# A recurrence stage without two-input work on GpSimd, and with its filler matmuls at fixed places

## The chip, the cores and the metric

The kernel runs on one core of a Trainium2 chip. The metric is the device time of one execution in microseconds (us); the median of three runs before the change is 2841.66 us (2840.65 to 2843.72). TensorE multiplies, VectorE, ScalarE and GpSimd work elementwise, and SyncE issues the DMAs. In rows of the profile they are PE (its weight loads PEld), DVE, ACT, POOL and SP.

## What is computed

One backbone layer over 1024 latent and 256 context tokens of width 1024: a half-step SwiGLU, two token mixers on one input projection, and a second half-step SwiGLU. The mixers are a softmax attention and a gated linear recurrence with 4 heads and two directions, over chunks of 64 tokens. The part that the change touches is the recurrence, cut here to what matters:

```python
def forget_gate(f_raw, lb):
    f = lb + (1.0 - lb) * sigmoid(f_raw)
    return 1.0 - f, log(f)                                  # k, g

b = cumsum(g, within each chunk)
ds = einsum('bnshk,bnshv->bnhkv', kc * exp(b_last - b), vc)  # per chunk
state = exp(b_last) * state + ds                             # from chunk to chunk
s = tril(einsum('bnchk,bnshk->bnhcs', qc * exp(b - b_mid), kc * exp(b_mid - b)))
o = einsum('bnhcs,bnshv->bnchv', s, vc) + einsum('bnchk,bnhkv->bnchv', qc * exp(b), s_prev)
o = rms_norm(o_forward + reversed(o_backward)) * silu(g_raw)
y = (sigmoid(p8) * (o_att @ w_att_out) + sigmoid(p9) * (o_hg @ w_hg_out)) @ w_o
```

## The kernel before

The layer runs as stages one behind another: first SwiGLU, input projections with attention, the recurrence stage, the merge of the two mixers, and second SwiGLU. Nearly all large products are done as three matmuls on a high and a low half of each operand (`term`, L98 to L102): a weight of 128x1024 is loaded by SyncE into one of three `st` buffers, `act.copy` makes the high half, and a subtraction makes the low half (`load_w`, L87 to L93). The engine of that subtraction (L92) is an argument.

The recurrence stage (L815 to L1040) takes each of 4 heads in 2 directions:

- `load_head` (L855 to L877) fetches a head's inputs and applies the sigmoids on ScalarE. GpSimd multiplies `g` by its sigmoid (L876).
- `prep` (L879 to L933) is the elementwise work of one direction: `fs` scaled on ScalarE (L880), `k` as one minus `fs` on GpSimd (L882), the logarithm on ScalarE, the scan on VectorE (L886 or L888), then exponentials on ScalarE and about fifteen products on VectorE, up to `b` (L930) and `qb` (L932).
- `mix` (L935 to L995) does the scores on TensorE (L941, L950), copies them under a mask into `ST` (L957), transposes (L968), forms chunk products (L977), and steps the state `Sp` on VectorE (L985), eight times one behind another.
- `head_out` (L997 to L1029) adds the two score tables on GpSimd (`both`, L1000), multiplies out the head's output on TensorE (L1008, L1010), normalises on VectorE, transposes (L1026), multiplies by `g` (L1028) and stores to `ohg_d`.

TensorE has little to do for a head itself. So the gate projections, which only the merge needs, are spread through the stage as fillers: 16 weight columns, each with two items of 24 matmuls of 128x512, 768 in all, written into `fb`, copied to `ft` on ScalarE and stored to `gate_d`. `Fillers.next` makes one item and asks for the weight of the next column; the pool of weight halves has 4 buffers, two columns. In the kernel before, `fill()` counts its calls and releases items in proportion (calls over 64); what is left is done by `fl.upto(1)` at the head of the merge stage. The tile framework orders the instructions of each engine from this program by priorities of its own; each engine then runs its own queue strictly in order.

The merge stage waits for both mixers: it reloads `oatt_d` and `ohg_d` through the same `st` buffers (L1060), splits them into halves (L1062, L1063), and multiplies with `w_mrg`.

Of the kernel before, what the change touches and what calls it, by code (L numbers as in the profile page):

```python
# [13 lines left out]
AF = mybir.ActivationFunctionType  # L14
ALU = mybir.AluOpType
# [37 lines left out]
def hybrid_block(ctx: ExitStack, tc: tile.TileContext, xT, cc, cols, w_mod, w_gate, w_up, w_down, w_tok, w_col,  # L53
# [765 lines left out]
    psF = out_ctx.enter_context(tc.tile_pool(name="ps3f", bufs=2, space=PSUM, reuse_waits="tile"))  # L819
    with tc.tile_pool(name="hg", bufs=1, reuse_waits="tile") as hp, \  # L820
            tc.tile_pool(name="psH", bufs=6, space=PSUM, reuse_waits="tile") as psH:
        fl = Fillers(wp, ep, psF, pool, False)
        for j in range(KT):
            fl.cols(B_GA, j, gate_d[0], (0, 1))
            fl.cols(B_GB, j, gate_d[1], (0, 1))
        calls = [0]

        def fill():
            calls[0] += 1
            fl.upto(calls[0] / 64)  # L830

        lower_bounds(hp.tile([P, 16], F32, name="lbr"))
        m01 = hp.tile([P, T + 1], BF16, name="m01")
# [21 lines left out]
        def load_head(h):  # L855
            rows = slice(h * P, (h + 1) * P)
            fs = []
            for d in range(2):
                t = hp.tile([P, T], F32, name="fs", bufs=3)
                sp.dma_start(out=t, in_=f_d[d][rows, :])  # L860
                fs.append(t)
            q = hp.tile([P, SEQ], F32, name="q", bufs=1)
            g = hp.tile([P, SEQ], F32, name="g", bufs=2)
            vt = hp.tile([P, NKT, P], F32, name="vt", bufs=2)
            sp.dma_start(out=q, in_=hq_d[rows, :])
            sp.dma_start(out=vt, in_=hv_d[:, rows].rearrange("(b p) d -> p b d", p=P))
            sp.dma_start(out=g, in_=hg_d[rows, :])
            table(fs[0], fs[0], AF.Sigmoid)
            sq = w4("sg", 1)
            table(sq, q, AF.Sigmoid)  # L870
            table(fs[1], fs[1], AF.Sigmoid)
            sg = w4("sg", 1)
            table(sg, g, AF.Sigmoid)
            tc.stamp_issue_order_token(act.preload_act_table_set("natural_log_exp_and_others").ins, "tables")
            dve.scalar_tensor_tensor(q, q, HG_SCALE, sq, op0=ALU.mult, op1=ALU.mult)
            pool.tensor_tensor(g, g, sg, op=ALU.mult)  # L876
            return fs, q, g, vt  # L877

        def prep(h, d, fs, q):  # L879
            act.activation(fs, fs, AF.Identity, scale=oml[:, d, h:h + 1], bias=lb[:, d, h:h + 1])  # L880
            k = hp.tile([P, T], F32, name="k", bufs=2)
            pool.tensor_scalar(k, fs, -1.0, 1.0, op0=ALU.mult, op1=ALU.add)  # L882
            table(fs, fs, AF.Ln)
            b = hp.tile([P, T], F32, name="b", bufs=2)
            if d == 0:
                dve.tensor_tensor_scan(b, m01[:, 0:T], fs, 0.0, op0=ALU.mult, op1=ALU.add)  # L886
            else:
                dve.tensor_tensor_scan(b[:, ::-1], m01[:, 1:T + 1][:, ::-1], fs[:, ::-1], 0.0,  # L888
                                       op0=ALU.mult, op1=ALU.add)
            mid, last = (31, 63) if d == 0 else (32, 0)  # L890
            b3 = b.rearrange("p (c t) -> p c t", t=CHUNK)
            x3 = b3[:, 0:16]
            fx = fs[:, 0:SEQ]
            dve.tensor_tensor(fx.rearrange("p (c t) -> p c t", t=CHUNK), x3,
                              x3[:, :, mid:mid + 1].broadcast_to([P, 16, CHUNK]), op=ALU.subtract)
            f, s_ = (0, 1) if d == 0 else (1, 0)

            dec = hp.tile([P, 52], F32, name="dec", bufs=2)
            em, el = dec[:, 20:36], dec[:, 36:52]
            dve.tensor_copy(dec[:, 0:20], b3[:, :, last])  # L900
            dve.tensor_copy(em, x3[:, :, mid])
            dve.tensor_tensor(el, dec[:, 0:16], em, op=ALU.subtract)
            bc = b3[:, 16:20]
            dve.tensor_tensor(bc, bc, dec[:, 16:20].unsqueeze(2).broadcast_to([P, 4, CHUNK]), op=ALU.subtract)
            act.activation(dec, dec, AF.Exp)
            qt = w4("qt")
            act.activation(qt, fx, AF.Exp)
            act.activation(fx, fx, AF.Exp, scale=-1.0)
            bx = b[:, SEQ:T]
            act.activation(bx, bx, AF.Exp, scale=-1.0)  # L910
            dec2 = hp.tile([P, 10], F32, name="dec2", bufs=2)
            dve.tensor_tensor(dec2, dec[:, 0:20:2], dec[:, 1:20:2], op=ALU.mult)
            dve.tensor_tensor(qt, qt, q, op=ALU.mult)
            dve.tensor_tensor(fx, fx, k[:, 0:SEQ], op=ALU.mult)
            dve.tensor_tensor(bx, bx, k[:, SEQ:T], op=ALU.mult)
            bf = bc[:, f::2]
            dve.tensor_tensor(bf, bf, dec[:, 16 + s_:20:2].unsqueeze(2).broadcast_to([P, 2, CHUNK]), op=ALU.mult)

            def wide(v, n):
                return v.unsqueeze(2).broadcast_to([P, n, CHUNK])  # L920

            k3, t3 = (t.rearrange("p (c t) -> p c t", t=CHUNK) for t in (fx, qt))
            q2 = hp.tile([P, 512], F32, name="q2", bufs=2)
            k1 = hp.tile([P, 512], F32, name="k1", bufs=2)
            dve.tensor_tensor(k1.rearrange("p (c t) -> p c t", t=CHUNK), k3[:, f::2], wide(el[:, f::2], 8), op=ALU.mult)
            dve.tensor_tensor(q2.rearrange("p (c t) -> p c t", t=CHUNK), t3[:, s_::2], wide(em[:, s_::2], 8),
                              op=ALU.mult)
            dve.tensor_tensor(el[:, f::2], el[:, f::2], dec[:, s_:16:2], op=ALU.mult)
            dve.tensor_tensor(em[:, s_::2], em[:, s_::2], dec[:, f:16:2], op=ALU.mult)
            dve.tensor_tensor(x3, k3, wide(el, 16), op=ALU.mult)  # L930
            qb = w4("qb", 3)
            dve.tensor_tensor(qb.rearrange("p (c t) -> p c t", t=CHUNK), t3, wide(em, 16), op=ALU.mult)  # L932
            return fx, qt, qb, b, q2, k1, dec2  # L933

        def mix(d, vt, fx, qt, qb, b, q2, k1, dec2):  # L935
            f, s_ = (0, 1) if d == 0 else (1, 0)
            ps = hbank()
            kr = slice(f * CHUNK, (f + 1) * CHUNK)
            for i in range(8):
# [46 lines left out]
                    state.append(nxt)  # L986

            kts = [to_tokens(groups[0])]
            fill()
            for j in range(3):  # L990
                if j < 2:
                    kts.append(to_tokens(groups[j + 1]))
                fill()
                update(groups[j], kts[j])
            return qb, Sp  # L995

        def head_out(h, vt, g, dirs):  # L997
            rows = slice(h * P, (h + 1) * P)
            both = hp.tile([P, 8, P], F32, name="both")
            pool.tensor_tensor(both, ST[0], ST[1], op=ALU.add)  # L1000
            ss = hp.tile([P, 8], F32, name="ss", bufs=2)
            pss = []
            for half in range(2):
                ps = hbank()
                for i in range(4):
                    bk = half * 4 + i
                    o = ps[:, i * P:(i + 1) * P]
                    pe.matmul(o, both[:, bk, :], vt[:, bk, :], start=True, stop=False)  # L1008
                    for d, (qb, Sp) in enumerate(dirs):
                        pe.matmul(o, qb[:, bk * P:(bk + 1) * P], Sp[:, bk, :], start=False, stop=(d == 1))  # L1010
                sq = hp.tile([P, 512], F32, name="sq", bufs=2)
                act.activation(sq, ps, AF.Square)
                dve.reduce_sum(ss[:, half * 4:half * 4 + 4], sq.rearrange("p (b e) -> p b e", e=P), axis=AX.X)
                pss.append((ps, sq))
            fill()
            r = hp.tile([P, 8], F32, name="rr", bufs=2)
            rsqrt(r, ss, P)
            for half, (ps, on) in enumerate(pss):
                dve.tensor_tensor(on.rearrange("p (b e) -> p b e", e=P), ps.rearrange("p (b e) -> p b e", e=P),
                                  r[:, half * 4:half * 4 + 4].unsqueeze(2).broadcast_to([P, 4, P]), op=ALU.mult)  # L1020
            fill()
            for half, (_, on) in enumerate(pss):
                cs_ = slice(half * 512, half * 512 + 512)
                ps = hbank()
                for i in range(4):
                    pe.transpose(ps[:, i * P:(i + 1) * P], on[:, i * P:(i + 1) * P], ident)  # L1026
                og = g[:, cs_]
                dve.scalar_tensor_tensor(og, ps, col[:, 120:121], og, op0=ALU.mult, op1=ALU.mult)  # L1028
                sp.dma_start(out=ohg_d[rows, cs_], in_=og)  # L1029

        for _ in range(4):
            fill()
        heads = [load_head(0)]
        ready = prep(0, 0, heads[0][0][0], heads[0][1])
        for h in range(HGH):
# [184 lines left out]
```

## Time and profile before

| | us |
|---|---|
| median of three runs | 2841.66 (2840.65 to 2843.72) |
| the profiled execution | 2842.11 |
| its span, first to last instruction | 2840.1 |
| PE busy | 2720.6 (96% of the span) |
| DVE busy | 1588.3 (56%) |
| ACT busy | 991.8 (35%) |
| POOL busy | 238.0 (8%) |

The mean granted TensorE clock is 0.985 of full speed. Busy shares are means over stages with different limits: the page's second part cuts the span into 40 slices of 71 us, and TensorE stands at nine tenths in most of them; in the three slices from about 1633 to 1846 us, inside the recurrence stage (about 1617 to 1902 us), it stands at eight, and VectorE at eight, eight and six. So the stage has to be read by itself.

### The profile page before, as it was taken

What the parts mean: (1) busy time and instruction counts of PE and PEld (TensorE: products, weight loads), DVE (VectorE), ACT (ScalarE), POOL (GpSimd) and SP (SyncE); (2) the same over time, 40 slices, a digit from 0 to 9 for tenths busy, and PEclk for the clock granted to TensorE, in tenths of its full rate; (3) what the DMA queues carried; (4) which work ended last, traced back from release to release, by engine and by line L of the source; (5) the groups of instructions that cost most, each with busy time, mean ns of one, the idle gap of its engine ahead of it and who ended that gap; (6) DMA issues with size and microseconds to landing.
All of it is one profiled execution on the core that took longest, in us unless ns stands there. A gap on an engine that the chain in (4) does not pass through costs nothing.

```text
span 2840.1 us, 37295 instructions
## 1 busy us (share of the span) xinstructions
PE 2720.6 (96%) x15032; PEld 2326.4 (82%) x15032; DVE 1588.3 (56%) x3053; ACT 991.8 (35%) x1463; POOL 238.0 (8%) x192
## 2 busy tenths in 40 slices
PE   4799999999999899999999988899999999999998
PEld 3588888888888798989988877788878888888887
DVE  7756544444434886566665488644495333333337
ACT  3521111111112443278776565344354211111122
POOL 4700000000000000200000132112000000000000
PEclk9899999999999999999999999999999999999999
DMA  6553223323211433311021333154353211111122
GB/s 230 178 160 90 76 73 89 97 76 96 62 43 56 145 116 112 99 45 36 29 66 34 93 131 127 65 192 138 115 175 115 70 45 45 45 52 52 45 79 92
DMA packets 115276, 261.56 MB, mean 92 GB/s; under 512 B 12320, under 2 KB 51872, under 8 KB 115104
## 3 DMA queue, kind: packets, MB, share of 16 engines
q1 hardware_dynamic: 115104, 259.18, 28.7%
q8 instruction: 118, 1.93, 0.3%
q14 instruction: 54, 0.44, 0.0%
HBM read 218.77 MB, written 40.37 MB: 91 GB/s over the span
## 4 chain that ended last, share of the span: by engine, by line
PE 82%; DVE 8%; issue 4%; ACT 3%; DMA 2%; POOL 1%; SPq 0%; DVEq 0%; ACTq 0%; POOLq 0%
PE bank L100 14%; PE bank L101 14%; PE bank L102 14%; PE y L100 6%; PE y L101 6%; PE y L102 6%; PE fb L102 3%; PE fb L101 3%; PE fb L100 3%; PE S L754 3%; PE bank L770 2%; PE po L783 1%; PE po L784 1%; PE qb L100 1%; PE qb L101 1%
## 5 line engine op out<-in xcount | busy, mean ns | idle before, releaser
L100 PE MATMUL bank<-uh,w 128*128 128x512 f32 (+1 forms) x1952 | 712.6, 366 | 19.9 <-ACT uh L457 15.0
L101 PE MATMUL bank<-ul,w 128*128 128x512 f32 (+1 forms) x1952 | 714.1, 366 | 6.8 <-POOL ul L458 6.8
L102 PE MATMUL bank<-uh,w 128*128 128x512 f32 (+1 forms) x1952 | 712.7, 365 | 0.3 <-DVE w L92 0.3
L91 ACT CAST w<-st 128x1024 fp32r<-128x1024 f32 x238 | 248.0, 1051 | 790.5 <-PE y L101 432.2
L100 PEld LDWEIGHTS bank<-uh,w 128*128 128x128 f32 x1952 | 369.1, 189 | 80.6 <-ACT uh L457 17.1
L101 PEld LDWEIGHTS bank<-ul,w 128*128 128x128 f32 x1952 | 369.6, 189 | 67.6 <-POOL ul L458 10.1
L102 PEld LDWEIGHTS bank<-uh,w 128*128 128x128 f32 x1952 | 370.2, 190 | 58.1 <-DVE w L92 0.8
L92 DVE TENSOR_TENSOR w<-st,w 128x1024 fp32r<-128x1024 f32 x216 | 263.8, 1230 | 239.7 <-ACT w L91 237.0
L352 DVE TENSOR_TENSOR y<-y,y 128x512 f32<-128x512 f32 (+1 forms) x416 | 254.8, 619 | 200.5 <-PE y L102 199.0
L100 PE MATMUL y<-h,w 128*128 128x512 f32 (+1 forms) x736 | 284.0, 388 | 10.8 <-DVE y L352 6.1
L101 PE MATMUL y<-h,w 128*128 128x512 f32 (+1 forms) x736 | 282.9, 385 | 0.0
L102 PE MATMUL y<-h,w 128*128 128x512 f32 (+1 forms) x736 | 281.5, 383 | 0.2
L337 DVE TENSOR_TENSOR sl<-bank,sl 128x512 f32<-128x512 f32 (+1 forms) x114 | 70.6, 620 | 369.8 <-PE bank L102 365.5
L100 PE MATMUL fb<-uh,w 128*128 128x512 f32 (+1 forms) x576 | 222.3, 386 | 0.3 <-ACT ft L112 0.3
L102 PE MATMUL fb<-uh,w 128*128 128x512 f32 (+1 forms) x576 | 219.6, 381 | 0.0
L101 PE MATMUL fb<-ul,w 128*128 128x512 f32 (+1 forms) x576 | 219.2, 380 | 0.0
L100 PEld LDWEIGHTS y<-h,w 128*128 128x128 f32 x736 | 139.1, 190 | 44.2 <-DVE y L352 10.0
L102 PEld LDWEIGHTS y<-h,w 128*128 128x128 f32 x736 | 139.5, 190 | 27.5 <-DVE w L92 1.0
L101 PEld LDWEIGHTS y<-h,w 128*128 128x128 f32 x736 | 139.8, 190 | 24.6 <-DVE h L339 0.2
L338 ACT CAST h<-sl 128x512 fp32r<-128x512 f32 (+1 forms) x92 | 55.3, 604 | 288.3 <-DVE sl L337 288.1
L336 ACT ACTIVATE sl<-bank 128x512 f32<-128x512 f32 (+1 forms) x114 | 61.2, 539 | 191.8 <-PE bank L102 191.3
L774 DVE TENSOR_TENSOR pl<-bank,ph 128x512 fp32r<-128x512 f32 x160 | 108.1, 684 | 29.4 <-ACT ph L773 29.4
(224 smaller groups left out, 4182.1 us busy)
## 6 DMA issues: line engine op xcount, KB each, us to landing
st<-in_w_mod SPq DMA_DIRECT2D x77, 512.0 KB, 3.7
st<-in_w_gate SPq DMA_DIRECT2D x56, 512.0 KB, 3.8
st<-in_w_up SPq DMA_DIRECT2D x56, 512.0 KB, 3.7
st<-in_w_down SPq DMA_DIRECT2D x56, 512.0 KB, 3.6
st<-in_w_col SPq DMA_DIRECT2D x36, 512.0 KB, 3.6
gate_d<-ft SPq DMA_DIRECT2D x32, 256.0 KB, 2.7
gt<-gate_d SPq DMA_DIRECT2D x32, 256.0 KB, 2.7
st<-in_w_o SPq DMA_DIRECT2D x16, 512.0 KB, 3.7
```

The costliest lines, as they stand in the source:

```text
L91: act.copy(hi, st)
L92: eng.tensor_tensor(lo, st, f32(hi), op=ALU.subtract)
L100: pe.matmul(ps, lh, rh, start=first, stop=False)
L101: pe.matmul(ps, lh, rl, start=False, stop=False)
L102: pe.matmul(ps, ll, rh, start=False, stop=last)
L336: act.activation(sl, pg, AF.Silu)
L337: dve.tensor_tensor(sl, pu, sl, op=ALU.mult)
L338: act.copy(hh, sl)
L352: dve.tensor_tensor(yd, py, yd, op=ALU.add)
L754: pe.matmul(S[:, cs_], qT[:, (s * 2 + t) * P:(s * 2 + t + 1) * P], kT[g][:, cs_], start=(s == 0), stop=(s == 1))
L770: pe.transpose(pt[:, (a * 2 + t) * P:(a * 2 + t + 1) * P], prob[t][:, kt * P:(kt + 1) * P], ident)
L774: dve.tensor_tensor(pl.rearrange("p a q -> p (a q)"), pt, f32(ph).rearrange("p a q -> p (a q)"), op=ALU.subtract)
```

## The change

Four operations of the recurrence stage leave GpSimd: the subtraction for filler weights (`Fillers` gets `dve`), the product `g`, and the sum `both` go to VectorE; `k` goes to ScalarE as an activation with scale -1 and bias 1. `fill` no longer counts; it makes one item, or as many as it is told. The calls stand at fixed places: four items ahead of the heads, one at the head of `mix`, one behind the masked copies, and two in `head_out` behind `both`. That is 4 + 16 + 8 = 28 items of 32; four remain for `fl.upto(1)`.

```diff
-        fl = Fillers(wp, ep, psF, pool, False)
+        fl = Fillers(wp, ep, psF, dve, False)
...
-        calls = [0]
-
-        def fill():
-            calls[0] += 1
-            fl.upto(calls[0] / 64)
+        def fill(n=1):
+            for _ in range(min(n, len(fl.todo))):
+                fl.next()
...
-            pool.tensor_tensor(g, g, sg, op=ALU.mult)
+            dve.tensor_tensor(g, g, sg, op=ALU.mult)
...
-            pool.tensor_scalar(k, fs, -1.0, 1.0, op0=ALU.mult, op1=ALU.add)
+            act.activation(k, fs, AF.Identity, scale=-1.0, bias=1.0)
...
         def mix(d, vt, fx, qt, qb, b, q2, k1, dec2):
             f, s_ = (0, 1) if d == 0 else (1, 0)
+            fill()
             ps = hbank()
...
             kts = [to_tokens(groups[0])]
-            fill()
             for j in range(3):
                 if j < 2:
                     kts.append(to_tokens(groups[j + 1]))
-                fill()
                 update(groups[j], kts[j])
...
-            pool.tensor_tensor(both, ST[0], ST[1], op=ALU.add)
+            dve.tensor_tensor(both, ST[0], ST[1], op=ALU.add)
+            fill(2)
...
-            fill()
             r = hp.tile([P, 8], F32, name="rr", bufs=2)
...
-            fill()
             for half, (_, on) in enumerate(pss):
...
-        for _ in range(4):
-            fill()
+        fill(4)
         heads = [load_head(0)]
```

How the queues change is shown at three places. On GpSimd, in the stage from the first head on, the kernel before has this (the first twelve rows of it; `w` is the low half of a filler weight):

```order
L876 TENSOR_TENSOR g<-g,sg 128x1024
L92 TENSOR_TENSOR w<-st,w 128x1024
L882 TENSOR_SCALAR k<-fs 128x1280
L92 TENSOR_TENSOR w<-st,w 128x1024
L876 TENSOR_TENSOR g<-g,sg 128x1024
L1000 TENSOR_TENSOR both<-ST_14480,ST_14481 128x1024
L882 TENSOR_SCALAR k<-fs 128x1280
L92 TENSOR_TENSOR w<-st,w 128x1024
L882 TENSOR_SCALAR k<-fs 128x1280
L92 TENSOR_TENSOR w<-st,w 128x1024
L876 TENSOR_TENSOR g<-g,sg 128x1024
L1000 TENSOR_TENSOR both<-ST_14480,ST_14481 128x1024
```

With the change, all that GpSimd has between the attention and the end of the merge is this:

```order
L832 MEMSET m_14470 128x1281
L842 MEMSET ST_14480 128x1024
L833 MEMSET m_14470 128x21
L842 MEMSET ST_14481 128x1024
L1077 TENSOR_TENSOR gt<-gt 128x512 x16
```

So GpSimd has no work at all beside the four heads. On VectorE, in the second head, behind the state of its first direction, the changed kernel has (`m` the chunk pattern of the scan, `s` and `Sp` the state, `dec` its decay):

```order
L874 TENSOR_TENSOR g<-g,sg 128x1024
L956 COPY_PREDICATED ST_14481<-mask_14474,hb 32x8x32
L884 SCALAR_TENSOR_TENSOR b<-m_14470,fs 128x1280
L997 TENSOR_TENSOR both<-ST_14480,ST_14481 128x1024
L892 TENSOR_TENSOR fs<-b 128x1024
L898 COPY dec<-b 128x20
L899 COPY dec<-b 128x16
L981 COPY s_15536<-hb 128x128
L900 TENSOR_TENSOR dec<-dec 128x16
L902 TENSOR_TENSOR b<-b,dec 128x256
L984 SCALAR_TENSOR_TENSOR Sp<-s_15536,dec_15191,hb 128x128
L92 TENSOR_TENSOR w<-st,w 128x1024
```

There `g`, `both` and a filler's `w` now stand between the steps of the next head's preparation and of the state. From the first scores to the last product by `g` of the first three heads VectorE's queue gets six, four and five of them (nine `w`, three `g`, three `both`).

On TensorE, at the outputs of the second head, the kernel before has (`fb` rows are fillers):

```order
L977 MATMUL hb<-vt,kt 128x128 x5
L1008 MATMUL hb<-vt,both 128x128
L1010 MATMUL hb<-Sp,qb 128x128
L1008 MATMUL hb<-vt,both 128x128
L1010 MATMUL hb<-Sp,qb 128x128
L100 MATMUL fb<-uh_91,w 128x512
L101 MATMUL fb<-ul_94,w 128x512
L102 MATMUL fb<-uh_91,w 128x512
L1010 MATMUL hb<-Sp,qb 128x128
L1008 MATMUL hb<-vt,both 128x128
L1010 MATMUL hb<-Sp,qb 128x128 x2
```

and with the change, behind 37 filler matmuls in one run:

```order
L1006 MATMUL hb<-vt,both 128x128
L1008 MATMUL hb<-Sp,qb 128x128
L1006 MATMUL hb<-vt,both 128x128
L1008 MATMUL hb<-Sp,qb 128x128 x2
L1006 MATMUL hb<-vt,both 128x128
L1008 MATMUL hb<-Sp,qb 128x128 x2
L1006 MATMUL hb<-vt,both 128x128
L1008 MATMUL hb<-Sp,qb 128x128 x2
```

So the fillers have moved ahead of the outputs. Counted over the whole stage, filler matmuls ahead of the first scores, in the four heads, and behind the last head's transposes are 138, 133, 108, 113, 132 and 144 before, and 139, 164, 123, 127, 138 and 77 with the change. TensorE's own recurrence matmuls are the same.

## Rows read from the trace of the kernel before

**Rows 1.** Page, part 1: busy time, share of the span, instructions.

```profile
PE 2720.6 (96%) x15032; PEld 2326.4 (82%) x15032; DVE 1588.3 (56%) x3053; ACT 991.8 (35%) x1463; POOL 238.0 (8%) x192
```

**Rows 2.** Busy time by stretch: length, then PE, PEld, DVE, ACT, POOL; clock; DMA.

```profile
1617.00:1653.20 36.20, 31.18 (x137) 25.15 (x136) 19.98 (x32) 24.64 (x29) 11.09 (x9) 0.99 0.69 228
1653.20:1715.70 62.50, 55.18 (x417) 47.14 (x418) 58.83 (x94) 35.39 (x43) 22.39 (x9) 0.90 0.32 108
1715.70:1767.90 52.20, 44.49 (x382) 38.42 (x380) 46.60 (x79) 28.70 (x36) 15.45 (x6) 0.93 0.33 109
1767.90:1823.40 55.50, 45.36 (x388) 39.22 (x386) 44.86 (x78) 22.84 (x32) 13.59 (x6) 0.94 0.25 84
1823.40:1870.60 47.20, 47.20 (x397) 41.02 (x395) 16.77 (x43) 11.62 (x20) 8.09 (x4) 1.00 0.18 62
1870.60:1902.10 31.50, 31.50 (x141) 26.06 (x139) 13.15 (x10) 17.68 (x23) 3.90 (x2) 1.00 0.83 275
```

**Rows 3.** PE's waits, 1640 to 1902 us: total, times, longest.

```profile
PE hb L1010 <- DVE Sp L985: 17.5, 4, 6.3
PE hb L1026 <- DVE sq L1019: 4.8, 3, 2.2
PE hb L941 <- DVE q L926: 4.7, 1, 4.7
```

**Rows 4.** Timeline of DVE and POOL: start, duration, engine, line; two clashes, one without.

```profile
1757.23 2.49 DVE L917 TENSOR_TENSOR b<-b,dec 128x128 f32<-128x128 f32 x1
...
1757.18 2.39 POOL L92 TENSOR_TENSOR w<-st,w 128x1024 fp32r<-128x1024 f32 x1 [10.64 <-ACT w L91]
...
1667.00 2.39 POOL L92 TENSOR_TENSOR w<-st,w 128x1024 fp32r<-128x1024 f32 x1 [8.06 <-ACT w L91]
...
1667.95 0.74 DVE L957 COPY_PREDICATED ST<-mask,hb 32x512 f32<-32x512 uint8 x1
```

**Rows 5.** Timeline of DVE: first and last lengthened instruction, each with its undisturbed like.

```profile
1654.43 3.39 DVE L932 TENSOR_TENSOR qb<-qt,dec 128x1024 f32<-128x1024 f32 x1
...
1664.70 1.21 DVE L932 TENSOR_TENSOR qb<-qt,dec 128x1024 f32<-128x1024 f32 x1
...
1816.44 0.17 DVE L196 SCALAR_TENSOR_TENSOR nw<-rr 128x8 f32<-128x8 f32 x1
...
1817.65 2.27 DVE L196 SCALAR_TENSOR_TENSOR nw<-rr 128x8 f32<-128x8 f32 x1
```

**Rows 6.** Groups of POOL, 1617 to 1902 us: busy, mean ns, idle before.

```profile
L92 POOL TENSOR_TENSOR w<-st,w 128x1024 fp32r<-128x1024 f32 x15 | 40.2, 2680 | 144.6 <-ACT w L91 116.7 <-PE hb L977 27.9
L882 POOL TENSOR_SCALAR k<-fs 128x1280 f32<-128x1280 f32 x8 | 14.1, 1768 | 20.3 <-ACT fs L880 17.5 <-issue 2.9
L1000 POOL TENSOR_TENSOR both<-ST,ST 128x1024 f32<-128x1024 f32 x4 | 9.5, 2375 | 11.3 <-DVE ST L957 11.3
```

**Rows 7.** Groups with the prices on the new engines: DVE in the whole span, ACT from 1560.

```profile
L92 DVE TENSOR_TENSOR w<-st,w 128x1024 fp32r<-128x1024 f32 x216 | 263.8, 1230 | 239.7 <-ACT w L91 237.0 <-issue 0.2
...
L880 ACT ACTIVATE fs<-fs,lb,oml 128x1280 f32<-128x1280 f32 x8 | 11.7, 1464 | 0.1
```

**Rows 8.** Timeline of PE: two filler matmuls, 15 apart.

```profile
1640.01 0.39 PE L102 MATMUL fb<-uh,w 128*128 128x512 f32 x1
...
1643.41 0.39 PE L102 MATMUL fb<-uh,w 128*128 128x512 f32 x1
```

**Rows 9.** Busy time by stretch, as in rows 2, behind the longest PE wait.

```profile
1742.90:1748.00 5.10, 4.98 (x22) 4.88 (x23) 5.10 (x6) 3.49 (x3) 1.26 (x1) 0.51 0.01 3
```

**Rows 10.** Timeline at the merge's head: last product by g, SP's loads, first w_mrg low half.

```profile
1869.18 1.41 DVE L1028 SCALAR_TENSOR_TENSOR g<-hb,col,g 128x512 f32<-128x512 f32 x2 [0.99 <-PE hb L1026]
...
1872.12 0.37 SPq L1060 DMA_DIRECT2D st<-oatt_d  x1
...
1892.63 2.60 SPq L88 DMA_DIRECT2D st<-in_w_mrg  x2
...
1898.13 1.23 DVE L92 TENSOR_TENSOR w<-st,w 128x1024 fp32r<-128x1024 f32 x1 [0.71 <-ACT w L91]
```

## The prediction

> **What bounds the kernel now.** The page comes first: TensorE is busy for 2720.6 of 2840.1 us [rows 1], so a change gains only where TensorE stands idle or runs slowly. The table by stretch shows where [rows 2]. Its stretches are: from the start of the gate fillers to the first scores (1653.2), the four heads, each up to the end of its last product by `g` (1715.7, 1767.9, 1823.4, 1870.6), and the rest up to the first matmul of the merge (1902.1). The reader is to see that the fourth head and the rest have no idle TensorE and a clock of 1.00, while the first three heads have 62.50 - 55.18 = 7.3, 7.7 and 10.1 us of idle, 25.2 us together, at a clock of 0.90 to 0.94. Ahead of them lie 5.0 us of idle.
>
> Then PE's waits: 17.5 us for the state `Sp`, 4.8 for the normalised output, 4.7 for the first head's `q`, all from VectorE [rows 3]. So in these heads VectorE is late: it is busy for 58.83 of 62.50, 46.60 of 52.20 and 44.86 of 55.50 us [rows 2].
>
> Why it is late shows in the timeline. A product of 128x128 takes 2.49 us, exactly while GpSimd makes a weight half in 2.39; a masked copy that reads PSUM takes its usual 0.74 beside just such a GpSimd instruction [rows 4]. Going through VectorE's instructions of the three heads, I found 15 that are longer than their undisturbed likes, the first 3.39 against 1.21, the last 2.27 against 0.17 [rows 5], each beside one on GpSimd. Excess by head: 10.9 us (2.2, 1.0, 1.6, 0.8, 2.2, 0.9, 2.2), 8.0 us (2.0, 1.8, 1.1, 0.9, 2.2) and 6.5 us (2.2, 2.2, 2.1), together 25.4 us. That is as much as TensorE's idle time there.
>
> The clock adds to it. Behind the longest wait (6.3 us, rows 3) the granted clock is 0.51, the lower of the two levels, 1.2 for 2.4 GHz [rows 9]. To price this: a filler matmul takes (1643.41 - 1640.01) / 15 = 0.227 us [rows 8]. The fourth head, with 132 of them and no loss, gives 47.2 - 132 x 0.227 = 17.3 us for a head's own matmuls. The first three heads, with 133, 108 and 113 fillers, should then take 47.5, 41.8 and 42.9 us, but TensorE is busy for 55.2, 44.5 and 45.4: another 12.9 us. So 38.1 us are lost in three heads.
>
> **The change, part by part.** The sum is made against the profiled execution, 2842.1 us, which lies 0.45 above the median of 2841.66.
>
> *GpSimd's work goes.* All 25.4 us of excess go with it: no instruction of GpSimd stands beside the heads any more. [...]
>
> *VectorE gets it.* In the three heads its queue gets six, four and five instructions of 128x1024 (nine `w`, three `g`, three `both`). GpSimd took 2.68 and 2.38 us for one [rows 6]; VectorE takes 1.23 for the same subtraction in other stages [rows 7], taken here for all: 7.4, 4.9 and 6.2 us, 18.5 together.
>
> *Each head, then*, is VectorE's busy time minus excess plus new work plus its own idle time, which I keep: 58.8 - 10.9 + 7.4 + 3.7 = 59.0; 46.6 - 8.0 + 4.9 + 5.6 = 49.1; 44.9 - 6.5 + 6.2 + 10.6 = 55.2. TensorE would need less: with 164, 123 and 127 fillers 54.5, 45.2 and 46.1 us. So VectorE still sets these heads, by 3 to 9 us each. The sum is 163.3 for 170.2: **-6.9 us**. In the third head VectorE's idle time lies between the second head's 5.6 and 10.6; much of it was waiting for TensorE, which has a state product behind a run of fillers there. I take the middle, 8.1: **-2.5 us**.
>
> *Fillers move ahead.* The third head's end has 138 + 77 = 215 behind it where 276 were. 61 x 0.227 = **-13.8 us**; this counts because the 60 that moved into the three heads fill waits and cost nothing as long as VectorE sets those heads. Without that cover they cost 13.6, all of the term.
>
> *The merge's head loses cover.* Before, from the last product by `g` (ends 1870.6) to the first low half of `w_mrg` (ends 1899.4) 28.8 us pass, with eight loads through the three `st` buffers [rows 10]: 3.6 us a load. 144 fillers hid it, until 1902.1. With the change 77 remain; TensorE starts on them 1.1 us before that product ends, so they cover 77 x 0.227 - 1.1 = 16.4 us. Three loads of `oatt_d` now stand ahead of the last `ohg_d` store in SP's queue, which leaves six: 6 x 3.6 = 21.6 us. **+5.2 us**; bounds 0 (loads at twice that pace) and 28.8 - 16.4 = 12.4.
>
> *`k` on ScalarE* costs at most 1.46 us each, the price of the scaling [rows 7]. ScalarE is busy for half of a head [rows 2], and `k` stood between the scaling and the logarithm before too, on GpSimd with 1.77 us on average [rows 6]. Taken as nothing; bounds -2 and +9 (six times 1.46 in the three heads). If ScalarE's slack were gone, the scan would be late by it.
>
> *Ahead of the first scores* VectorE gets one more `w` and `g`. TensorE already waits 5.0 us there, so this is no cover for it: between +2.7 (a `w` and a `k` in the chain) and -2. Taken as nothing. Two further `w` come into the last attention unit; the 5.0 us of idle behind it take them up.
>
> Sum: -6.9 - 2.5 - 13.8 + 5.2 = **-18.0 us**, 2824 us.
>
> **The rivals.**
> *Everything comes back.* If VectorE's waits shrink as its queue gets free, TensorE sets all heads and the 38.1 us go whole: 2804 us. For it: TensorE's need of 54.5, 45.2 and 46.1 lies near VectorE's bare work of 55.3, 43.5 and 44.6. Against: the two have to wait for each other several times a head. Chance 0.15.
>
> *The merge waits in full*, 12.4 in place of 5.2: 2831 us. For it: the DMA share is 0.83 in that stretch, the highest of the six [rows 2]. Chance 0.18.
>
> *A wash.* The fillers in front of its products make VectorE wait longer, the three heads stay at 170.2, and the merge's wait eats 12.4 of the 13.8: 2841 us. Chance 0.09.
>
> *Slower: fillers wait for VectorE.* GpSimd stood ready for `w`: before it, it was idle for 116.7 us waiting for ScalarE's half [rows 6]. In the queue of VectorE, which is busy for 94% of the first head, `w` comes only when what stands ahead is done, and TensorE runs in order, so a filler without its weight holds up the recurrence behind it. Two or three instructions ahead make 3.0 us; nine weights give +27 on -18: 2851 us. It decides from 18.0 / 9 = 2.0 us a weight. Against it: a column's two items take 48 x 0.227 = 10.9 us, and the next weight is asked for one column ahead. Chance 0.08.
>
> That the change does not do what it says is excluded by the queues: GpSimd's is empty there, and VectorE's has the work.
>
> **How the numbers follow.** 0.50 for the forecast, 0.15, 0.18, 0.09 and 0.08 for the rivals. About 0.2% (5.7 us) is what a measurement of this kernel can tell from no change. Faster: 0.50 + 0.15 + 0.18 = 0.83; within: the wash, 0.09; slower: 0.08. The range holds the first three, with 0.83: 2804 from full recovery, up to 2837, which is the merge's full wait and half of `k`'s upper bound on top of it.
>
> **What would show it.** POOL without two-input work from 1617 us on, and no VectorE instruction of 128x1024 or less over about 1.3 us there. The three heads at about 59, 49 and 53 us. Clock in them above 0.94. The longest wait for `Sp` under 3 us. A TensorE wait of some 5 us at the merge's first matmul, for `w_mrg` or `h`. The forecast is wrong if the heads stay near 170 us together, if `fb` matmuls wait for DVE `w`, or if stages outside 1617 to 1950 us change.

## The result and the profile after

The changed kernel takes 2816.78 us (median of four runs, 2814.09 to 2818.98) where the kernel before takes 2841.15 beside it: 24.4 us less, ratio 0.9913 with a 95% interval of 0.9896 to 0.993. A second set of four runs gave 2816.68. The forecast was 2824.0 with a range of 2804 to 2837: the side and the range held, and the gain was a third larger than forecast. The profiled execution took 2814.09 us, its span is 2812.3; it is the fastest of its four, which matters where sums from its profile are set beside the medians.

The page's first part, to be read against [rows 1]: TensorE's and VectorE's busy times have hardly moved. What went is time in which TensorE stood.

```profile
PE 2717.0 (97%) x15032; PEld 2320.6 (83%) x15032; DVE 1588.1 (56%) x3077; ACT 999.7 (36%) x1471; POOL 162.4 (6%) x160
```

The busy time by stretch, as in [rows 2], from the last matmul of the attention to ten microseconds into the merge: ahead of the first scores, the four heads up to the end of each last product by `g`, the rest up to the merge's first matmul, and the merge's first 10 us (after the length: PE, PEld, DVE, ACT, POOL, then clock and DMA).

```profile
1614.60:1648.80 34.20, 31.81 (x142) 26.02 (x140) 18.47 (x30) 26.82 (x29) 0.00 (x0) 1.00 0.76 245
1648.80:1707.70 58.90, 57.51 (x449) 48.66 (x450) 57.08 (x105) 40.88 (x51) 0.00 (x0) 0.97 0.38 120
1707.70:1755.00 47.30, 46.06 (x397) 38.78 (x395) 43.13 (x82) 31.74 (x39) 0.00 (x0) 1.00 0.40 127
1755.00:1805.10 50.10, 48.27 (x400) 41.25 (x398) 44.00 (x82) 24.65 (x34) 0.00 (x0) 0.97 0.30 97
1805.10:1854.40 49.30, 48.91 (x403) 41.62 (x402) 21.70 (x48) 10.71 (x18) 0.00 (x0) 1.00 0.22 72
1854.40:1874.40 20.00, 16.75 (x75) 13.55 (x73) 9.70 (x10) 14.85 (x19) 0.00 (x0) 1.00 0.91 308
1874.40:1884.40 10.00, 10.00 (x37) 8.12 (x38) 6.13 (x6) 3.59 (x4) 1.39 (x1) 0.83 0.71 241
```

The reader is to see three things. The first three heads have 1.4, 1.2 and 1.8 us without TensorE where there were 25.2 together, and a clock of 0.97, 1.00 and 0.97. GpSimd is empty up to the merge. And the loss has a new place: 3.3 us of idle ahead of the merge, with a clock of 0.83 behind it.

TensorE's waits, 1640 to 1902 us, say the same [rows 3]: the wait for `Sp` fell from 17.5 to 3.7 us, and the second entry is new.

```profile
PE hb L1008 <- DVE Sp L984: 3.7, 3, 1.8
PE bank L100 <- ACT w L91: 3.3, 1, 3.3
PE hb L940 <- DVE q L924: 2.4, 1, 2.4
PE hb L976 <- ACT kt L970: 0.7, 2, 0.5
PE hb L1022 <- DVE sq L1016: 0.4, 1, 0.4
```

VectorE's groups in the stage (count, busy, mean ns, idle before): none holds a lengthened instruction any more. The 128x128 product by `dec`, 2.49 us in the clash of [rows 4] and 0.558 in the mean of its eight before, is at 0.289. All 15 low halves of filler weights cost what the same line cost elsewhere [rows 7].

```profile
L92 DVE TENSOR_TENSOR w<-st,w 128x1024 fp32r<-128x1024 f32 x15 | 18.4, 1224 | 20.8 <-ACT w L91 12.6 <-DMA vt<-hv_d 5.5 <-PE hb L967 2.8
L884 DVE TENSOR_TENSOR_SCAN b<-m,fs 128x1280 f32<-128x1280 bf16 x4 | 11.3, 2825 | 2.6 <-ACT fs L851 2.5
...
L892 DVE TENSOR_TENSOR fs<-b 128x1024 f32<-128x1024 f32 x8 | 9.8, 1223 | 0.1
...
L915 DVE TENSOR_TENSOR b<-b,dec 128x128 f32<-128x128 f32 x8 | 2.3, 289 | 0.0
...
L898 DVE COPY dec<-b 128x20 f32<-128x20 f32 x8 | 1.4, 177 | 0.0
```

### The profile page after: what moved, and what is told of

Its sections match the earlier page's. It is cut to its first block, busy times and chain, and to the rows that moved or that the text cites. A ratio compares the mean times of both kernels' runs of the same rounds, so it can differ in the third digit from the quotient of the medians.

```text
span 2812.3 us, 37276 instructions
## 1 busy us (share of the span) xinstructions
PE 2717.0 (97%) x15032; PEld 2320.6 (83%) x15032; DVE 1588.1 (56%) x3077; ACT 999.7 (36%) x1471; POOL 162.4 (6%) x160
## 3 DMA queue, kind: packets, MB, share of 16 engines
q1 hardware_dynamic: 115104, 259.18, 28.9%
## 4 chain that ended last, share of the span: by engine, by line
PE 85%; DVE 7%; ACT 3%; issue 2%; DMA 2%; POOL 0%; SPq 0%; DVEq 0%; ACTq 0%; POOLq 0%
PE bank L100 14%; PE bank L101 14%; PE bank L102 14%; PE y L100 7%; PE y L101 6%; PE y L102 6%; PE fb L102 3%; PE fb L101 3%; PE fb L100 3%; PE S L754 3%; PE bank L770 2%; PE po L783 1%; PE po L784 1%; PE qb L100 1%; PE qb L101 1%
## 5 line engine op out<-in xcount | busy, mean ns | idle before, releaser
L92 DVE TENSOR_TENSOR w<-st,w 128x1024 fp32r<-128x1024 f32 x232 | 285.1, 1237 | 256.7 <-ACT w L91 246.1
```

The source lines that it names most:

```text
L92: eng.tensor_tensor(lo, st, f32(hi), op=ALU.subtract)
```

## The experiments

**One measure for all of them.** Runs that put different numbers of fillers into the heads can't be compared by the heads' lengths. So each stretch is compared with what TensorE needs for it, by the two prices of the prediction: 0.227 us a filler [rows 8] and 17.3 us for a head's own matmuls. Fillers are counted in TensorE's order, up to the last transposes of a head. Loss in the three heads = their length minus 0.227 times their fillers minus 3 x 17.3. Before: 170.2 - 354 x 0.227 - 51.9 = 37.9. After: 156.3 - 414 x 0.227 - 51.9 = 10.4. Ahead of the first scores (from the attention's last matmul) and behind the fourth head only the fillers are subtracted; behind the last head the first of them start about a microsecond early, so -1 there means no loss. In no profile does the fourth head lose more than 1.0. The column "lengthened" is worked out from VectorE's groups in the stage: count times the mean's excess over the same group in the second profile of the changed kernel. All in us; one profile each.

| kernel | ahead | three heads | behind | lengthened | median | ratio to before, 95% |
|---|---|---|---|---|---|---|
| before | 5.6 | 37.9 | -1.2 | 29.5 | 2841 to 2843 | |
| changed | 2.6 | 10.4 | 2.4 | 0.8 | 2816.78 | 0.9913 (0.9896 to 0.993) |
| changed, second set | 2.6 | 8.0 | 3.7 | 0.0 | 2816.68 | 0.9909 (0.9894 to 0.9924) |
| 1: engines alone | 5.2 | 11.8 | -1.2 | 0.0 | 2815.76 | 0.9914 (0.99 to 0.9927) |
| 2: filler places alone | 5.1 | 32.5 | 3.6 | 31.3 | 2843.19 | 1.0005 (0.9996 to 1.0014) |
| 3: `w` back | 6.1 | 25.3 | 2.5 | 18.5 | 2835.75 | 0.9976 (0.9967 to 0.9985) |
| 4: `k` back | 2.9 | 15.9 | 2.3 | 3.6 | 2824.38 | 0.9938 (0.9926 to 0.9951) |
| 5: `g` and `both` back | 2.6 | 19.5 | 2.3 | 6.2 | 2828.79 | 0.9951 (0.9938 to 0.9963) |
| 6: GpSimd work added | 5.8 | 28.9 | 2.7 | 21.8 | 2842.33 | 1.0005 (0.9996 to 1.0014) |
| 7: six items kept | 2.6 | 7.9 | -1.0 | -0.2 | 2812.00 | 0.9897 (0.9882 to 0.9913) |
| 8: merge weight first | 2.6 | 8.6 | -1.0 | | 2813.54 | 0.9899 (0.9885 to 0.9912) |
| 9: less VectorE work | 2.7 | 7.4 | 2.6 | 0.4 | 2815.86 | 0.9906 (0.9889 to 0.9922) |
| 10: 7 and 8 together | 2.6 | 7.8 | -1.0 | | 2813.82 | 0.9896 (0.9881 to 0.9911) |

### 1. The engines alone, 2. the filler places alone

Kernel 1 is the kernel before with the four operations on the new engines and with `fill()` counting its calls as it did:

```diff
-        fl = Fillers(wp, ep, psF, pool, False)
+        fl = Fillers(wp, ep, psF, dve, False)
...
-            pool.tensor_tensor(g, g, sg, op=ALU.mult)
+            dve.tensor_tensor(g, g, sg, op=ALU.mult)
...
-            pool.tensor_scalar(k, fs, -1.0, 1.0, op0=ALU.mult, op1=ALU.add)
+            act.activation(k, fs, AF.Identity, scale=-1.0, bias=1.0)
...
-            pool.tensor_tensor(both, ST[0], ST[1], op=ALU.add)
+            dve.tensor_tensor(both, ST[0], ST[1], op=ALU.add)
```

> The four operations leave GpSimd as in the change, the fillers keep the counted calls of the kernel before. Theory 'ports' (VectorE was held up by GpSimd's two-input instructions, and that is what TensorE waited for): no lengthened VectorE instruction, the first three heads take about 59, 49 and 53 us instead of 62.5, 52.2 and 55.5 (-9.4), 250 instead of 276 filler matmuls are left behind the third head in the order (-5.9), and the merge keeps its cover of 144: 2826 us (2822 to 2830). Theory 'places' (the fixed places of the fillers bring the gain): the three heads stay near 170 us, 2841 us (2838 to 2844).

Kernel 2 is the changed kernel with those four lines turned back, so only the fillers' places differ from before.

> The fillers as in the change, all four operations on GpSimd as before. Theory 'ports': VectorE's instructions are lengthened by 20 us or more in the first three heads, these stay near 170 us together; 220 instead of 276 filler matmuls behind the third head (-12.7) and a wait of some 5 us at the merge: 2834 us (2829 to 2840). Theory 'places': 2822 us or less, with the three heads near 156 us.

Measured: 2815.76 us for the engines alone, 2843.19 for the places alone. Each lies on the side that the theory of the ports gives, and outside its range: kernel 1 is 6 us faster than 2822, the low end, and kernel 2 is 3 us slower than 2840, the high end. The engines alone bring the whole gain, and the fixed places alone bring nothing: in kernel 2 VectorE's instructions are lengthened by 31.3 us (29.5 before), the heads lose 32.5, and the shorter cover behind them leaves a wait of 4.4 us at the merge on top. With the engines moved the places can bring something: kernel 7 below, which has them and no wait at the merge, is 3.8 us below kernel 1, and the ranges of four runs don't meet (2810.46 to 2813.55 against 2814.11 to 2818.8). In kernel 1 the fillers went forward by themselves: 157, 122 and 113 of them lie in the three heads instead of 133, 108 and 113, under calls that are the same as before. TensorE's queue is ordered by the framework, and with other engines behind the operations it comes out another way.

Kernel 1 is also the one in which the mechanism of the slower rival shows most (kernel 6 has 1.2 us of it and kernel 4 0.3). TensorE's two longest waits, 1640 to 1902 us:

```profile
PE hb L1010 <- DVE Sp L985: 5.5, 4, 2.5
PE fb L102 <- DVE w L92: 2.2, 1, 2.2
```

Fillers waited once for VectorE's `w`, 2.2 us, not nine times, and this was ahead of the first scores.

### 6. GpSimd work added that the layer does not ask for

Does the clash do it, or the other order of the queues that came with it? Kernel 6 leaves TensorE's, VectorE's and ScalarE's queues of the changed kernel row for row as they are, and gives GpSimd 16 products of 128x1024, two behind each `k` (they raise `k` to a higher power):

```diff
             act.activation(k, fs, AF.Identity, scale=-1.0, bias=1.0)
+            for _ in range(2):
+                pool.tensor_tensor(k[:, 0:SEQ], k[:, 0:SEQ], k[:, 0:SEQ], op=ALU.mult)
```

> The changed kernel with two added GpSimd products k = k*k of 128x1024 per preparation (16 in all, so the output's k is raised to the fourth power and the result is not the reference's); the queues of TensorE and VectorE are the same, row for row. Theory 'ports': the 12 added instructions beside the first three heads lengthen VectorE's instructions by about 1.7 us each (25.4 us by 15 in the kernel before), +20 us, where scans and products of 128x1024 run beside them; 2835 us (2826 to 2845). Theory 'places' or any that leaves the ports out: 2817 us (2814 to 2820), no VectorE instruction over 1.3 us but the scans at 2.8.

Measured: 2842.33 us. The whole gain is gone, at 25.6 / 16 = 1.6 us for each added instruction. GpSimd's only group in the stage, and four of VectorE's in that kernel (count, busy, mean ns, idle before):

```profile
L882 POOL TENSOR_TENSOR k<-k 128x1024 f32<-128x1024 f32 x16 | 45.9, 2866 | 134.7 <-ACT k L880 134.0
...
L894 DVE TENSOR_TENSOR fs<-b 128x1024 f32<-128x1024 f32 x8 | 16.5, 2059 | 0.1
...
L914 DVE TENSOR_TENSOR fs<-fs,k 128x1024 f32<-128x1024 f32 x8 | 9.7, 1216 | 0.0
L900 DVE COPY dec<-b 128x20 f32<-128x20 f32 x8 | 9.3, 1167 | 0.0
...
L999 DVE TENSOR_TENSOR both<-ST,ST 128x1024 f32<-128x1024 f32 x4 | 6.5, 1627 | 0.1
```

The reader of GpSimd's result, `fs<-fs,k`, has no idle time ahead of it: VectorE never waits for the added work by a semaphore, and no other engine has a wait that names GpSimd. What it pays is inside its own instructions, 2.06 for 1.22 us and 1.17 for 0.18, together 21.8 us. TensorE pays 5.8 - 2.6 = 3.2 us more ahead of the first scores and 28.9 less 8.0 to 10.4 in the heads. Its longest waits show how it gets there, 1620 to 1880 us:

```profile
PE hb L978 <- ACT kt L972: 9.2, 4, 3.9
PE hb L1010 <- DVE Sp L986: 6.7, 3, 2.8
PE hb L942 <- DVE q L926: 5.6, 1, 5.6
```

The first of them names ScalarE (0.7 us in the changed kernel). But from 1640 to 1830 us ScalarE waits 20.3 us for VectorE's lengthened `fs<-b`, 9.5 in the changed kernel, and its queue, like the others, is in the same order in both. That the later `kt` is a consequence of this is likely and not shown by itself. So GpSimd's work beside VectorE is enough for a loss of the size that was removed; this is shown, since no instruction of the other three engines was moved.

### 3, 4 and 5. One part back on GpSimd

Each is the changed kernel with one part turned back: the low half of filler weights (3), `k` (4), or `g` and `both` (5).

```diff
-        fl = Fillers(wp, ep, psF, dve, False)
+        fl = Fillers(wp, ep, psF, pool, False)
```

> The changed kernel with only the subtraction for filler weights back on GpSimd. Theory 'ports, by the rows of the kernel before': seven of the 15 lengthened VectorE instructions stood beside such a subtraction, with 15.0 us of excess; VectorE in turn is spared nine subtractions of 1.23 us, 11.1 us; VectorE has 3.9 us more in the first three heads: 2821 us (2818 to 2826). Theory 'fillers wait for VectorE's half' (the rival that ended slower): faster than the changed kernel, 2812 us or less. If the weights alone made the gain: 2832 us or more.

> The changed kernel with only k back on GpSimd (one input). By the rows of the kernel before, 4.7 us of the excess stood beside it, and ScalarE is spared eight activations of about 1.3 us: 2821 us (2817 to 2825) if VectorE sets the heads; 2814 us or less if ScalarE's added activations cost more than the ports give.

> The changed kernel with g and both back on GpSimd. By the rows of the kernel before, 5.8 us of the excess stood beside both and none beside g, and VectorE is spared six instructions of 1.22 us in the first three heads, 7.3 us: a wash, 2815 us (2812 to 2820). If any two-input GpSimd instruction costs the 1.5 to 2 us that the added ones did in the run before this: 2822 us or more.

Measured: 2835.75, 2824.38 and 2828.79 us, that is +19.0, +7.6 and +12.0 on the changed kernel. All three cost more than I expected from the excess that lay beside each kind of instruction in the trace of before. Kernel 4 is still inside its range (2817 to 2825); kernels 3 and 5 are far above theirs and came out where their last alternatives had put them, at 2832 or more and 2822 or more. The sum of the three, 38.6, is more than the 26.4 that all three cost together in kernel 2, so the parts don't add up. Why is not shown; each edit also changes where the other instructions fall.

How `w` comes to 19 us is seen in the timeline of kernel 3, VectorE and GpSimd (start, duration):

```profile
1679.10 1.22 DVE L892 TENSOR_TENSOR fs<-b 128x1024 f32<-128x1024 f32 x1
...
1680.49 2.11 DVE L898 COPY dec<-b 128x20 f32<-128x20 f32 x1
...
1679.25 3.32 POOL L92 TENSOR_TENSOR w<-st,w 128x1024 fp32r<-128x1024 f32 x1 [11.62 <-DMA gate_d<-ft]
```

GpSimd begins 0.15 us behind a two-input product of VectorE, which keeps its 1.22; GpSimd's takes 3.32 for the usual 2.39, nearly as if it had waited the product out. Then a copy of 20 columns, 0.17 us by itself, takes 2.11 and ends (1682.60) with GpSimd's instruction (1682.57). Three of the eight such copies are held like this and lose 6.0 us, one of them ahead of the first scores; in all of the stage 18.5 us are lost, 3.3 of them in two mask casts at its very start. No engine has a wait in this stage that names GpSimd. The copy stands in `prep`, between the scan and the exponentials, so the next state and the next scores are made from what stands behind it.

Kernel 5 is not clean evidence on the clash. Its VectorE instructions are lengthened by only 6.2 us. In its three heads VectorE's scan waits 4.7 us for ScalarE's `fs` (1.1 in the changed kernel, 3.3 in the kernel before), and ScalarE waits 6.0 us for the load of `q`. With `g` and `both` on GpSimd the framework orders the loads and ScalarE's work another way, and that may be a part of the 12.0; I did not separate it.

### 9. Less work on VectorE

Does VectorE's length set the heads, as the forecast has it? Kernel 9 takes twelve instructions of 128x1024 out of its three heads: the product `g`, and the low half of filler weights.

```diff
-            dve.tensor_tensor(g, g, sg, op=ALU.mult)
...
-                box.append(load_w(self.wp, w_col[blk + j], KT, self.eng))
+                    hi = self.wp.tile([P, 1024], R, name="w")
+                    act.copy(hi, st)
+                    box.append((hi.rearrange("p (a b) -> p a b", a=KT),) * 2)
```

> The changed kernel with twelve instructions of 128x1024 fewer in VectorE's queue from the first scores to the third head's last product by g: the product g by its sigmoid is left out (g is used raw), and the low halves of filler weights are not made (the high half stands in their place, TensorE's matmuls are as many as before). VectorE sets the heads (the step of the forecast): 12 x 1.23 us = 14.8 us less VectorE work, and the first three heads fall from 156 us to what TensorE needs by the forecast, about 146 us together; time about 2807. Rival, TensorE and chains of waits set the heads and VectorE's new work fills gaps: the three heads stay above 152 us and the time within 4 us of the changed kernel's 2816.8.

Measured: 2815.86 us, 0.8 below the changed kernel on the same chip, where the first theory said ten less. Busy time of the three heads by stretch (DVE is the third busy time):

```profile
1652.80:1703.80 51.00, 49.70 (x417) 42.95 (x418) 49.16 (x95) 38.02 (x46) 0.00 (x0) 0.97 0.42 142
1703.80:1752.00 48.20, 46.59 (x394) 39.46 (x392) 40.97 (x79) 32.66 (x41) 0.00 (x0) 1.00 0.43 135
1752.00:1803.20 51.20, 50.23 (x413) 42.32 (x410) 39.41 (x79) 24.05 (x34) 0.00 (x0) 1.00 0.28 96
```

VectorE is busy for 129.5 us instead of 144.2, so 14.7 of work are gone, and it is idle for 20.9 instead of 12.1: most of what was taken out became waiting. The three heads are 150.4 long, under the 152 that the rival named, but thirteen fillers (3.0 us) have moved out of them, eight ahead of the first scores and five into the fourth head; by the loss, 7.4 against 8.0 to 10.4, the removal bought 0.6 to 3.0 us, and the whole run gained 0.8. The rival holds: with GpSimd gone, VectorE's length no longer sets these heads.

### 7, 8 and 10. The wait at the merge

The tail of the stage, SyncE's loads, ScalarE, VectorE and TensorE in the timeline of the changed kernel [rows 10]:

```profile
1868.83 0.34 SPq L88 DMA_DIRECT2D st<-in_w_mrg  x1
...
1873.26 1.04 ACT L91 CAST w<-st 128x1024 fp32r<-128x1024 f32 x1 [0.53 <-DMA st<-in_w_mrg]
...
1874.34 1.23 DVE L92 TENSOR_TENSOR w<-st,w 128x1024 fp32r<-128x1024 f32 x1 [0.35 <-ACT w L91]
...
1870.72 0.39 PE L102 MATMUL fb<-uh,w 128*128 128x512 f32 x1
...
1874.36 0.50 PE L100 MATMUL bank<-h,w 128*128 128x512 f32 x1 [3.25 <-ACT w L91]
...
1878.34 0.40 PE L100 MATMUL bank<-h,w 128*128 128x512 f32 x1
```

The last filler is done at 1871.1, the merge's first matmul starts at 1874.36, when the first high half of `w_mrg` is there. Behind that, ten matmuls take 3.98 us where they would take 2.27 at 0.227: the engine had stood for 3.25 us, the granted clock is 0.83 in the next ten microseconds, and 1.7 us more are lost. Two remedies: keep six items for the stage's end, by leaving out the two in the last head's second direction (7), or load the first weight of the merge ahead of the reloads (8).

```diff
-            dirs.append(mix(1, vt, *nxt))
+            dirs.append(mix(1, vt, *nxt, more=h + 1 < HGH))
```

```diff
+        first = load_w(wp, w_mrg[0], KT)
...
-            wh, wl = load_w(wp, w_mrg[d], KT)
+            wh, wl = load_w(wp, w_mrg[d], KT) if d else first
```

> The changed kernel, but the last direction of the last head calls no filler: 90 instead of 138 matmuls in the fourth head, 125 instead of 77 behind it. If the merge's wait (3.3 us in the changed kernel, and the lower clock behind it) comes from cover that is too short and the fourth head has no use for its fillers: the wait goes, 2812 us (2809 to 2815). If the fourth head needs them to cover the steps between TensorE, ScalarE and VectorE: the same waits come back there, 2817 us (2815 to 2822).

> The changed kernel, with the first weight of the merge loaded ahead of the mixers' outputs. The changed kernel's TensorE waits 3.3 us at the merge for that weight's high half on ScalarE, the last of six loads behind the last store. If the load's place in the queue is the cause: the wait falls to under 2 us, 2813 us (2811 to 2816). If the outputs of the recurrence arrive no earlier than that weight did, or its load pushes them back: the wait passes to them, 2817 us (2815 to 2820).

> The changed kernel with both remedies for the merge's wait: no fillers in the last head's second direction, so that six are left for the stage's end, and the first weight of the merge loaded ahead of the reloads. Theory (each alone removes the one wait of 3.3 us and the slow clock behind it, and nothing else is late there): no more than either alone, 2812 to 2814. Rival (the tail still hides a part of the loading that TensorE then waits for further into the merge): 2 to 4 us below either alone, about 2809.

> The changed kernel itself, unedited, on the same chip as the two others, so that both remedies are compared with it in one place. Expected: 2815 to 2818 us, 3 to 5 us above the kernel with both remedies. If it lies within 1.5 us of that kernel, the gain seen from the remedies was the difference of chips and runs.

Measured: 2812.00, 2813.54 and 2813.82 us, and 2816.68 for the changed kernel beside the last. The wait is gone in all three; with both remedies TensorE's waits of the stage are

```profile
PE hb L1010 <- DVE Sp L986: 3.5, 3, 1.8
PE hb L941 <- DVE q L924: 2.4, 1, 2.4
PE hb L978 <- ACT kt L972: 1.1, 2, 0.6
PE po L784 <- DVE pl L774: 1.0, 1, 1.0
PE hb L1024 <- DVE sq L1018: 0.6, 2, 0.4
```

The two don't add up, since each alone removes the one wait. On one chip the kernel with both is 2.9 us faster than the changed kernel, where 3 to 5 were expected and under 1.5 would have made the gain a difference of chips and runs; the ranges of four runs don't meet (2811.12 to 2814.6 against 2816.17 to 2818.82); that is 0.1%, less than the bound of the prediction, and the intervals of the ratios to before overlap. Kernel 7 has the lowest median, 29.9 us below before on its chip.

## Why the prediction held, and where it was off

By the measure above the forecast was: three heads -6.9 - 2.5, and 60 fillers taken in (13.6), a loss of 23.0 less; +5.2 at the merge; nothing elsewhere. The profile of the changed kernel has -27.5 in the three heads, -3.0 ahead of them, +3.6 up to the merge and +1.7 of slow clock behind it, +0.7 in the fourth head: -24.5. The medians differ by 24.4, but that the two agree so closely is luck. The two profiled executions differ by 27.8 us in their spans: the stage, up to the merge's first matmul, is 26.0 shorter, 1.7 lie ahead of it, and from that matmul to the end they take the same 938.0, slow clock included. In the second set's profile the stage is 27.2 shorter and the rest 4.0 longer. So outside the stage single executions differ by a few us either way.

**GpSimd's work goes: right.** VectorE's busy time in the three heads was to be 55.3, 43.5 and 44.6 us; it is 57.1, 43.1 and 44.0. So the excess did go and the new work did cost its 1.23 us each. Kernel 6 shows that work on GpSimd beside VectorE is enough to bring the loss back, and kernel 3 brings back 19.0 of the 24.4 us with the one part that had most of the excess beside it. Not all of the loss before was this: there TensorE also waited 2.0 us for `both` and ScalarE 3.5 us for `k` by semaphores, both of GpSimd, which the prediction left out; what these were worth was not measured apart.

**VectorE's own idle time, "which I keep": wrong in size.** It was kept at 3.7, 5.6 and 8.1 us, 17.4 together, and is 12.1: 1.8, 4.2 and 6.1. These 5.3 us are the larger part of what the forecast missed. In the three heads its waits for TensorE fell from 10.5 to 6.0 us and those for ScalarE from 6.9 to 3.5. VectorE had waited for TensorE, which had waited for VectorE. The rival in which everything comes back named this mechanism; the truth lies between, with 8.0 to 10.4 of the 38.1 us left.

**"So VectorE still sets these heads": wrong.** Kernel 9 took 14.7 us of its work away and got at most 3.0. Adding up an engine's busy time gave nearly the right heads (156.3 us, forecast 160.8), but it isn't what bounds them, so that the forecast came this near is in part luck. In the table, the loss over the changed kernel (heads and ahead; its heads at 9.2, the mean of its two profiles) is 0.8 to 1.1 times the lengthening in kernels 2, 3, 6 and before, and 1.7 and 1.9 times in 5 and 4, where other waits came along; plain work taken away brought about a fifth of its length at most (3.0 of 14.7). A likely reason, argued and not shown, is that a lengthened copy between scan and exponentials delays the next state, while the product `g` and a filler's `w` have slack.

**Fillers move ahead, -13.8: right as a sum, wrong as a term of the change.** I counted it for the fixed places. Kernel 1 has the old calls and the same time; kernel 2 has the fixed places and none of it. A filler in a head saves its 0.227 us only where the head would else wait, and that was already in the heads' loss.

**The merge's head: right.** Six loads at 3.6 us were to bring the first low half 21.6 us behind the last product by `g`; it came after 1875.57 - 1854.41 = 21.2. TensorE started 1.2 us earlier, with the high half alone, and so waited 3.3, not 5.2; the slow clock behind that wait, which I had left out here, makes it 5.0. The second set shows 4.5 for the wait. The rival in which it waits in full (12.4) did not come.

**Ahead of the first scores, 0 with bounds of -2 and +2.7: off, and outside.** It lost 5.6 before and 2.6 now. With `w` back it is 6.1, with GpSimd's work added 5.8, with `k` or with `g` and `both` back 2.9 and 2.6. So it was the clash with GpSimd there too, which I had looked for in the heads alone: TensorE's wait for the first head's `q` is 4.7 us before, 5.9 and 5.6 in kernels 3 and 6, and 2.4 in the changed kernel. The 5.2 of kernel 1 has another source: the fillers' waits for `w`, 2.2 us for the low half and 0.9 for the high half, lie there, at a clock of 0.95.

**`k` on ScalarE, 0: right as a price.** TensorE's waits for ScalarE in the heads come to 0.7 us, all for `kt`.

**The upper end of the range.** The merge's full wait and half of `k`'s bound come to 2831 + 4.5 = 2835.5, not 2837. Nothing hung on it.

## What to carry to other kernels

Before giving GpSimd "free" elementwise work beside a busy VectorE, compare the durations of VectorE's small instructions with their undisturbed likes; if some are ten times as long, moving the work onto VectorE itself can be cheaper, though it adds to the busier engine. Price such a clash at its microseconds or more (0.8 to 1.9 times here), by what stands behind the lengthened instruction, and price added work by the gaps it can fall into. When a stage gets shorter its cover for the next stage's loads gets shorter too: look at the first wait behind it, and keep a few fillers or start one load earlier.

## What the runs showed that I had not expected

**A copy with one input waits for GpSimd too.** I had thought of the instructions that wait as ones with two inputs in SBUF. The copy of 128x20 took 2.11 us beside GpSimd's `w` (kernel 3) and 1.17 in the mean of eight in kernel 6, for 0.18. One of the 15 of the kernel before was such a copy too, the 1.1 us in the second head's excess:

```profile
1735.91 1.24 DVE L900 COPY dec<-b 128x20 f32<-128x20 f32 x1
...
1734.87 2.24 POOL L882 TENSOR_SCALAR k<-fs 128x1280 f32<-128x1280 f32 x1
```

The Trainium skill ("SBUF — State Buffer", Who interferes with whom) says that a VectorE instruction with at most one SBUF input does not contend with GpSimd as long as it is outside the modes that use two ports, and lists copies among those that can enter one. These rows agree with that exception; whether this copy ran in such a mode no run here shows.

**Sixteen instructions of one engine cost the kernel 25 us with no wait for that engine anywhere.** In kernel 6 the waits that grew are for VectorE and ScalarE, and none names GpSimd; where the time starts, only the mean durations of VectorE's groups show.
